# Block sums of the second MLP matrix moved into the first matrix's stage, and the first token group issued earlier

## The chip, the cores and the metric

The kernel runs on one core of one Trainium2 chip. The metric is the device time of one execution in microseconds. A core has TensorE (PE, matmuls; PEld is its weight load), VectorE (DVE), ScalarE (ACT), GpSimd (POOL) and SyncE (SP). In this kernel all transfers are issued on SP's queue, which issues them in order. Data lie in SBUF; matmuls write to PSUM, which has eight banks.

## The reference, cut to what matters

The kernel computes two layers of a token mixer, each followed by a dense MLP; the change is in the MLP and in what stands right before it.

```
def _sqrelu_mlp(h, w1, w2):
    return jnp.square(jax.nn.relu(h @ w1)) @ w2
...
for i in range(DEPTH):                       # DEPTH = 2
    ...                                      # mixer: short convolution (layer 0), mLSTM (layer 1)
    x = x + mx[2] * _rmsnorm(yx, nw[1])
    x = x + mx[5] * _rmsnorm(_sqrelu_mlp(_modulate(_rmsnorm(x, nw[2]), mx[3], mx[4]), mlp_w1[i], mlp_w2[i]), nw[3])
    if not last:
        ...                                  # the same for 256 context tokens
```

The model width is 1024, the MLP's inner width 4096. Layer 0 works on 1280 tokens (256 of context and 1024), layer 1 on 1024. All inputs are 32-bit floats.

## The kernel before

Every operand of a large matmul is split into a high and a low part (`fp32r`): ScalarE casts the value (the high part), VectorE subtracts the cast from it (the low part), and each product is three matmuls (`PASSES`: high-high, high-low, low-high). `piece` (L119) does this for a 128 x 512 weight piece: a cast at L122 and a subtraction at L123. The results go round a ring of eight slots.

Both MLP matrices use a 2 x 2 block product with seven block multiplications instead of eight (products numbered 1 to 7, used in the order 1, 6, 5, 7, then 2, 3, 4 in the first matrix's stage and 1, 6, 5, 7, 4, 2, 3 in the second's). For four of them (4, 5, 6, 7) the weight operand is a sum or difference of blocks of the matrix, and the activation operands are sums as well.

`out_proj` (L355) is the stage ahead of the MLP. For each tile of 128 tokens it multiplies by the output matrix, adds the normed result to the residual stream (`post_norm`, L283) and normalises again. For each pair of tiles `pre_norm2` (L323) transposes the result, applies scale and shift, forms the block sums (`sums`, L318 to L321) and writes the split parts into A0 or A1, the operands of the first MLP stage. A0 holds the first token group (384 token pairs in layer 0, 256 in layer 1), A1 the second (256). A1 lies where the output matrix lay, so the last two pairs' writes (`left`) are run after the stage.

`mlp_up` (L403) is the first matrix's stage. It takes the 4096 columns in 16 blocks q. For each it loads two tiles of w1 (512 KB each), forms four sums (L415, L416, L420, L425) in tiles `tw`, makes seven pieces, and for each of the two token groups runs seven products of 12 matmuls into the banks X, Y, Z, W. The banks are evicted by ScalarE (L447, L457) and VectorE (L449 to L459), squared-ReLU is applied on ScalarE, and VectorE forms the activation's four block sums. The tile `st` with seven parts goes to `hid_d` in DRAM (L465).

`mlp_down` (L468) is the second matrix's stage. For each of the seven products it makes a pass over 16 blocks k of w2's rows: `w_piece` loads blocks of w2 into a tile `raw` and, for products 4 to 7, forms the sum on VectorE (L485 for product 5, L490 and L491 for 6, L496 for 7, L500 for 4); product 6 stores its sum to `t2_d`, from which product 4 starts. `h_piece` loads the activation part from `hid_d` (`hr`, two buffers) and splits it (L509, L510). One step multiplies the piece with all token pairs (L515): five pairs in layer 0, four in layer 1, each into a PSUM bank of its own. At a pass's end `evict` empties the banks; there are six of them. The norms that follow (`done`, `finish`) are worked off between the steps.

The order of instructions on each engine and of DMAs on SP is fixed at build time by a scheduler: it follows program order where the operands of an instruction are expected to be ready. SBUF tiles lie in pools on two stacks, left and right; a tile in a newly opened pool waits until the older tiles at its address are no longer used. `raw` tiles come from a pool of three.

Of the kernel before, what the change touches and what calls it, by code (L numbers as in the profile page):

```python
# [37 lines left out]
def hybrid_kernel(  # L38
# [46 lines left out]
    t2_d = tc.dram_tile([2, DFF // P // 2, P, 512], F32, name="t2_d")  # L85
# [196 lines left out]

    def post_norm(ys, xsrc, G, T):  # L283
        xt = T.tile([P, D], F32, tag="xt", name="xt", bufs=hold["xt"])
        nc.sync.dma_start(xt, xsrc)
        tt = T.tile([P, D], F32, tag="tmp", name="tt", bufs=hold["tt"])
# [10 lines left out]
        return xt, tt  # L297
# [25 lines left out]
    def pre_norm2(xns, t, l, T, tp):  # L323
# [3 lines left out]
        def rest(A, c0):  # L327
            for k0 in range(0, 4, 2):
                val = T.tile([P, 4, 2, P], F32, tag="xt", name="val2", bufs=hold["xt"])
                S = T.tile([P, 4, 2, P], F32, tag="xt", name="S2", bufs=hold["xt"])  # L330
                for kk in range(2):
# [16 lines left out]
                for src, i0, n in ((val, 0, 3), (S, 3, 4)):  # L348
                    d = A[:, i0 : i0 + n, :, k0 : k0 + 2, c0 : c0 + P]
                    nc.scalar.copy(d[:, :, 0], src[:, 0:n])  # L350
                    nc.vector.tensor_sub(d[:, :, 1], src[:, 0:n], d[:, :, 0].bitcast(F32))
# [3 lines left out]
    def out_proj(l, zsrc, held, wsrc, tiles, xsrc, xdst, T, Z, acc, tp, G, A, early):  # L355
        ws = [load_w(wsrc[k * P : (k + 1) * P, :]) for k in range(KD)]
        later, xns, left = None, [], []
        hold.update(xt=3, tt=4)
        for t in tiles:
# [23 lines left out]
            xt, tt = post_norm(ps, xsrc(t), G(t), T)  # L383
# [7 lines left out]
            if len(xns) == 2:  # L391
                i = (t - tiles[0]) // 2
                rest = pre_norm2(xns, t - 1, l, T, tp)
# [5 lines left out]
        return later, left  # L399
# [3 lines left out]
    def mlp_up(l, As, M, acc):  # L403

        for q in range(NQ):
            raw = []
            for j in range(2):
                r = rawp.tile([P, 1024], F32, tag="raw", name="raw")
                nc.sync.dma_start(r, w1[l, 2 * q + j])
                raw.append(r)  # L410
            (b11, b21), (b12, b22) = [(r[:, 0:512], r[:, 512:1024]) for r in raw]
            ts = lambda: M.tile([P, 512], F32, tag="tw", name="tw", bufs=3)
            w = {1: piece(b11)}
            t1, t2 = ts(), ts()
            nc.vector.tensor_sub(t1, b12, b11)  # L415
# [754 lines left out]
```

## Time and profile before

| | us |
|---|---|
| median of three runs | 2706.17 (2695.35 to 2712.82) |
| the profiled execution's own time | 2706.2 |
| its span, first to last instruction | 2704.4 |
| TensorE busy in the span | 2577.7 (95%) |
| VectorE, ScalarE busy | 1665.5 (62%), 1157.0 (43%) |
| first MLP stage, layers 0 and 1 (with the change-over before it) | 532 to 953, 1982 to 2331 |
| second MLP stage, layers 0 and 1 | 953 to about 1390, 2331 to 2704 |

The busy time of TensorE is that of overlapping matmuls with modelled ends, so 95% does not say that it runs at its best rate; the number of matmuls in a stretch says more. PEclk is the granted clock of TensorE as a share of full speed.

### The profile page before, as it was taken

The page shows a single profiled execution, that of the slowest core. Times are in us where ns is not written, and L with a number is a line of the kernel's source. Part 1 is how long each engine was busy: PE and PEld are TensorE (multiplying, and loading weights), DVE is VectorE, ACT ScalarE, POOL GpSimd, SP SyncE. Part 2 cuts the span into 40 slices and gives each one's busy share as a digit, 9 for nine tenths or more (in the row PEclk, how much of TensorE's full clock was granted, in tenths as well). Part 3 has the DMA queues.
Part 4 walks back from the last instruction along what each step waited for, and adds up shares of the span by engine and source line. Part 5 has one row for each costly group of instructions (what it writes and reads, how often), then busy time and mean ns, then how long its engine had stood idle before and what let it go on. Part 6 is the DMA issues. An engine that isn't in the chain of part 4 may idle for free.

```text
span 2704.4 us, 38658 instructions
## 1 busy us (share of the span) xinstructions
PE 2577.7 (95%) x14520; PEld 2235.4 (83%) x14520; DVE 1665.5 (62%) x3020; ACT 1157.0 (43%) x2529; POOL 98.1 (4%) x223
## 2 busy tenths in 40 slices
PE   8999999989999998999999999999979999988998
PEld 6888787789999976787888778787869999866776
DVE  6677875665565555766657553544566666556765
ACT  6211113554444432435554543435555555423343
POOL 1000001100000000001020000000100000000010
PEclk9999999989999999999999999799989999989999
DMA  7466644333443388876633222213424444678875
GB/s 285 130 195 188 207 145 132 126 97 118 150 146 125 120 268 253 286 244 220 218 104 81 70 67 59 57 42 95 131 84 141 138 153 144 210 251 272 260 244 191
DMA packets 225021, 435.97 MB, mean 161 GB/s; under 512 B 17226, under 2 KB 108666, under 8 KB 224834
## 3 DMA queue, kind: packets, MB, share of 16 engines
q1 hardware_dynamic: 224834, 433.51, 50.1%
q8 instruction: 114, 1.87, 0.3%
q14 instruction: 73, 0.60, 0.1%
HBM read 333.07 MB, written 100.16 MB: 160 GB/s over the span
## 4 chain that ended last, share of the span: by engine, by line
PE 52%; issue 30%; DMA 9%; DVE 6%; ACT 2%; POOL 1%; SPq 0%; DVEq 0%; POOLq 0%; ACTq 0%
PE op L374 7%; PE psd L515 7%; PE psZ L432 4%; PE psW L432 4%; PE psX L432 4%; PE psv L842 4%; PE pso L129 3%; DMA raw<-in_w_dram 3%; DMA mraw<-in_mod_w_dram 3%; PE psc L129 3%; DMA Dm<-nm_d 2%; PE psb L129 2%; PE psu L129 2%; PE psY L432 2%; PE po L1009 1%
## 5 line engine op out<-in xcount | busy, mean ns | idle before, releaser
L515 PE MATMUL psd<-w,hp 128*128 128x512 f32 x3024 | 735.2, 404 | 47.6 <-ACT w L122 25.4
L515 PEld LDWEIGHTS psd<-w,hp 128*128 128x128 f32 x3024 | 579.2, 193 | 199.9 <-ACT w L122 31.5
L122 ACT CAST w<-raw 128x512 fp32r<-128x512 f32 x320 | 197.0, 619 | 225.7 <-DVE raw L491 67.8
L123 DVE TENSOR_TENSOR w<-raw,w 128x512 fp32r<-128x512 f32 x320 | 218.7, 688 | 98.3 <-ACT w L122 94.2
L509 ACT CAST hp<-hr 128x512 fp32r<-128x512 f32 (+1 forms) x226 | 150.6, 669 | 237.1 <-DMA hr<-hid_d 128.5
L432 PE MATMUL psX<-A,w 128*128 128x256 f32 (+1 forms) x1536 | 229.2, 298 | 14.3 <-ACT p L447 14.3
L432 PE MATMUL psZ<-A,w 128*128 128x256 f32 (+1 forms) x1536 | 228.2, 298 | 0.0
L432 PE MATMUL psW<-A,w 128*128 128x256 f32 (+1 forms) x1536 | 226.5, 297 | 0.0
L432 PEld LDWEIGHTS psX<-A,w 128*128 128x128 f32 x1536 | 213.6, 190 | 15.1 <-ACT p L447 15.1
L510 DVE TENSOR_TENSOR hp<-hr,hp 128x512 fp32r<-128x512 f32 (+1 forms) x226 | 168.5, 749 | 88.7 <-ACT hp L509 87.6
L432 PEld LDWEIGHTS psZ<-A,w 128*128 128x128 f32 x1536 | 214.4, 190 | 0.0
L432 PEld LDWEIGHTS psW<-A,w 128*128 128x128 f32 x1536 | 212.8, 189 | 0.0
L374 PE MATMUL op<-w,zs 128*128 128x512 f32 x864 | 205.4, 397 | 2.0 <-ACT zs L368 1.8
L374 PEld LDWEIGHTS op<-w,zs 128*128 128x128 f32 x864 | 162.0, 189 | 38.9 <-ACT zs L368 2.5
L220 DVE SCALAR_TENSOR_TENSOR macc<-mraw,sil,macc 128x1024 f32<-128x1024 f32 x112 | 140.4, 1280 | 39.6 <-DMA mraw<-in_mod_w_dram 39.3
L462 ACT ACTIVATE st<-st 128x256 f32<-128x256 f32 (+1 forms) x128 | 56.9, 445 | 224.9 <-DVE st L453 179.7
L109 ACT CAST w<-raw 128x1024 fp32r<-128x1024 f32 (+1 forms) x73 | 75.4, 1039 | 161.7 <-PE psc L129 54.9
L842 PE MATMUL psv<-w,hT 128*128 128x256 f32 (+1 forms) x960 | 142.3, 301 | 0.9 <-ACT val L270 0.9
L842 PEld LDWEIGHTS psv<-w,hT 128*128 128x128 f32 x960 | 128.2, 198 | 7.5 <-issue 1.8
L110 DVE TENSOR_TENSOR w<-raw,w 128x1024 fp32r<-128x1024 f32 (+1 forms) x73 | 87.6, 1208 | 70.5 <-ACT w L109 70.2
L432 PE MATMUL psY<-A,w 128*128 128x256 f32 (+1 forms) x768 | 116.9, 302 | 2.4 <-ACT w L122 2.4
L129 PE MATMUL psc<-hT,w 128*128 128x512 f32 (+1 forms) x576 | 114.4, 350 | 0.6 <-DVE hT L279 0.4
(241 smaller groups left out, 3582.0 us busy)
## 6 DMA issues: line engine op xcount, KB each, us to landing
raw<-in_w_dram SPq DMA_DIRECT2D x128, 512.0 KB, 4.7
raw<-in_w_dram SPq DMA_DIRECT2D x224, 256.0 KB, 3.9
hid_d<-st SPq DMA_DIRECT2D x48, 896.0 KB, 4.1
mraw<-in_mod_w_dram SPq DMA_DIRECT2D x80, 512.0 KB, 4.0
hr<-hid_d SPq DMA_DIRECT2D x104, 320.0 KB, 3.6
hr<-hid_d SPq DMA_DIRECT2D x122, 256.0 KB, 3.7
hid_d<-st SPq DMA_DIRECT2D x16, 1344.0 KB
xd<-xt SPq DMA_DIRECT2D x26, 512.0 KB, 2.7
```

Of the source, the lines that this page charges most:

```text
L109: nc.scalar.copy(w[0], src)
L110: nc.vector.tensor_sub(w[1], src, w[0].bitcast(F32))
L122: nc.scalar.copy(w[:, 0], src)
L123: nc.vector.tensor_sub(w[:, 1], src, w[:, 0].bitcast(F32))
L129: nc.tensor.matmul(ps, w[a][:, k * P : (k + 1) * P], hold["hT"][:, k, b, t0 : t0 + n], start=(k == 0 and i == 0), stop=(k == KD - 1 and i ...
L220: nc.vector.scalar_tensor_tensor(ac[v], raw, s, ac[v], ALU.mult, ALU.add)
L374: nc.tensor.matmul(ps[h], zs[:, a, k, :], ws[k][b][:, h * 512 : (h + 1) * 512], start=(k == 0 and i == 0), stop=(k == KD - 1 and i == 2),)
L432: nc.tensor.matmul(ps, w[i][:, a, k * P : (k + 1) * P], A[:, PIECE[i], b, k, :], start=(first and k == 0 and j == 0), stop=(k == 3 and j = ...
L509: nc.scalar.copy(h[:, 0], r)
L510: nc.vector.tensor_sub(h[:, 1], r, h[:, 0].bitcast(F32))
L515: nc.tensor.matmul(ps, h[:, a, o : o + P], w[:, b], start=(first and j == 0), stop=(last and j == 2))
L842: nc.tensor.matmul(ps[:, 0 : self.g], hold["hT"][:, k, a_, t * P : (t + 1) * P], self.wv[k // self.per][b_][:, k % self.per * self.g : (k ...
```

## The change

The first matrix's stage gets a second task. After each block q a new function `down_sums` loads the four blocks k = q of w2 (two tiles of 512 KB, one buffer each), forms the four sums for products 4 to 7 on VectorE and stores them to DRAM (`t_d`, 1 MB per block). `w_piece` in the second stage then only loads 256 KB, from w2 or from `t_d`, and makes the piece. `hr` has three buffers instead of two.

`mlp_up` is cut into `up_weights`, `up_group` and `down_sums`. The first block's first token group is issued before the `left` writes into A1; these now work on half-size tiles (m=1: one instead of two feature blocks at a time) in two buffers of a pool X of their own. The temporaries of that first group (pool M0) lie where `out_proj`'s pool T lay, which is closed earlier, since the normed tiles (`tt`) now lie in X. In `up_weights` two of the four sums are written over the loaded blocks, and `tw` has two buffers. In `up_group` the temporaries p1, u2, u4 and c21 are parts of `st`. In the last block the second group is run before the first.

```
-            for k0 in range(0, 4, 2):
-                val = T.tile([P, 4, 2, P], F32, tag="xt", name="val2", bufs=hold["xt"])
-                S = T.tile([P, 4, 2, P], F32, tag="xt", name="S2", bufs=hold["xt"])
-                for kk in range(2):
+            for k0 in range(0, 4, m):
+                val, S = [pl.tile([P, 4, m, P], F32, tag=tag, name=nm) for nm in ("val2", "S2")]
+                for kk in range(m):
...
+            tt = X.tile([P, D], F32, tag="xn", name="tt", bufs=4)
+            xt = post_norm(ps, xsrc(t), G(t), T, tt)
...
-                    later = lambda rest=rest, i=i: rest(A, i * P)
+                    later = lambda rest=rest, i=i: rest(A, i * P, T, "xt", 2)
                 else:
-                    left.append(lambda A, rest=rest, i=i: rest(A, (i - early) * P))
+                    left.append(lambda A, rest=rest, i=i: rest(A, (i - early) * P, X, "vs", 1))
...
+    def up_weights(l, q, M):
...
+        t2, t3 = [M.tile([P, 512], F32, tag="tw", name="tw", bufs=2) for _ in range(2)]
+        w = {1: piece(b11)}
+        nc.vector.tensor_sub(t3, b22, b12)
+        nc.vector.tensor_sub(b12, b12, b11)
+        nc.vector.tensor_sub(t2, b22, b12)
+        w[6] = piece(t2)
+        w[5] = piece(b12)
+        w[7] = piece(t3)
+        w[2] = piece(b21)
+        w[3] = piece(b22)
+        nc.vector.tensor_sub(b21, b21, t2)
+        w[4] = piece(b21)
...
+    def up_group(l, q, w, A, n, c0, M, acc):
...
+        st = M.tile([P, 7, n], F32, tag="st7", name="st7")
+        r11, r12, r22, c21, u2 = [st[:, i] for i in (0, 1, 2, 5, 6)]
...
+        prod(X, 1, True)
+        nc.scalar.copy(u2, X)
+        prod(Y, 6, True)
+        add(u2, Y, u2)
...
+    def down_sums(l, k, M):
+
+        r = []
+        for j in range(2):
+            r.append(M.tile([P, 1024], F32, tag=f"rw{j}", name="rw", bufs=1))
+            nc.sync.dma_start(r[j], w2[l, (2 * k + j) * P : (2 * k + j + 1) * P, :])
+        (b11, b12), (b21, b22) = [(x[:, 0:512], x[:, 512:1024]) for x in r]
+        t3 = M.tile([P, 512], F32, tag="tw", name="t3", bufs=2)
+        sub = nc.vector.tensor_sub
+        sub(t3, b22, b12)
+        sub(b12, b12, b11)
+        sub(b22, b22, b12)
+        sub(b21, b21, b22)
+        nc.sync.dma_start(t_d[l, k, :, 3], t3)
+        nc.sync.dma_start(t_d[l, k, :, 2], b12)
+        nc.sync.dma_start(t_d[l, k, :, 0:2], r[1].rearrange("p (a b) -> p a b", a=2))
+
+    def mlp_up(l, As, sX, left, acc):
+
+        (A0, n0), (A1, n1) = As
+        with pool("M0", bufs=1, side="right") as M:
+            w = up_weights(l, 0, M)
+            up_group(l, 0, w, A0, n0, 0, M, acc)
+            for f in left:
+                f(A1)
+        sX.close()
+        with pool("M", bufs=2, side="right") as M:
+            up_group(l, 0, w, A1, n1, n0, M, acc)
+            down_sums(l, 0, M)
+            for q in range(1, NQ):
+                w = up_weights(l, q, M)
+                both = [(A0, n0, 0), (A1, n1, n0)]
+                for A, n, c0 in both if q < NQ - 1 else both[::-1]:
+                    up_group(l, q, w, A, n, c0, M, acc)
+                down_sums(l, q, M)
...
         def w_piece(i, k):
-            raw = lambda: rawp.tile([P, 1024], F32, tag="raw", name="raw2")
             row = lambda j: w2[l, (2 * k + j) * P : (2 * k + j + 1) * P, :]
-            r = raw()
-            if i in (1, 2, 3):
...
-            o = r[:, 512:1024]
-            if i == 5:
-                nc.sync.dma_start(r, row(0))
-                nc.vector.tensor_sub(o, o, r[:, 0:512])
-            elif i == 6:
-                nc.sync.dma_start(r, row(0))
-                e = raw()[:, 0:512]
-                nc.sync.dma_start(e, row(1)[:, 512:1024])
-                nc.vector.tensor_sub(o, e, o)
-                nc.vector.tensor_add(o, o, r[:, 0:512])
-                nc.sync.dma_start(t2_d[l, k], o)
...
-            return piece(o)
+            src = {1: row(0)[:, 0:512], 2: row(1)[:, 0:512], 3: row(1)[:, 512:1024]}
+            r = rawp.tile([P, 1024], F32, tag="raw", name="raw2")[:, 0:512]
+            nc.sync.dma_start(r, src[i] if i in src else t_d[l, k, :, {4: 0, 6: 1, 5: 2, 7: 3}[i]])
+            return piece(r)
...
-            r = H.tile([P, NP * P], F32, tag="hr", name="hr", bufs=2)[:, 0:n]
+            r = H.tile([P, NP * P], F32, tag="hr", name="hr", bufs=3)[:, 0:n]
```

## Rows read from the trace of the kernel before

**Rows 1.** Busy time of each engine on the page, whole span, share and instructions
```profile
PE 2577.7 (95%) x14520; PEld 2235.4 (83%) x14520; DVE 1665.5 (62%) x3020; ACT 1157.0 (43%) x2529; POOL 98.1 (4%) x223
```

**Rows 2.** Stretches: start:end, length, busy of each engine, clock, DMA share, GB/s; first stage
```profile
582.00:952.00 370.00, 370.00 (x2512) 370.00 (x2511) 216.54 (x429) 176.72 (x371) 0.00 (x0) 1.00 0.40 134
...
2028.00:2330.00 302.00, 302.00 (x2519) 302.00 (x2519) 199.97 (x430) 165.71 (x373) 0.00 (x0) 1.00 0.45 147
```

**Rows 3.** Stretches of the second matrix's stage, both layers
```profile
953.30:1253.50 300.20, 284.60 (x1190) 225.24 (x1190) 182.51 (x269) 109.68 (x174) 0.00 (x0) 0.98 0.79 258
...
1017.00:1085.00 68.00, 57.89 (x230) 43.89 (x231) 35.32 (x51) 19.80 (x33) 0.00 (x0) 0.97 0.82 258
...
2330.60:2602.50 271.90, 244.37 (x967) 191.60 (x966) 170.27 (x265) 101.24 (x174) 0.00 (x0) 0.94 0.80 257
...
2335.00:2345.00 10.00, 10.00 (x31) 7.83 (x32) 3.81 (x6) 2.80 (x5) 0.00 (x0) 0.70 0.78 246
...
2382.00:2453.00 71.00, 54.51 (x190) 40.23 (x189) 37.30 (x56) 19.75 (x34) 0.00 (x0) 0.88 0.78 244
...
2506.00:2554.00 48.00, 46.60 (x192) 37.11 (x192) 35.01 (x56) 20.35 (x34) 0.00 (x0) 0.96 0.84 275
...
2554.00:2602.50 48.50, 46.58 (x192) 37.01 (x192) 33.33 (x53) 20.58 (x36) 0.00 (x0) 0.96 0.74 234
...
2562.00:2602.00 40.00, 40.00 (x174) 32.35 (x172) 24.83 (x40) 17.94 (x32) 0.00 (x0) 1.00 0.79 251
```

**Rows 4.** Waits in 2382 to 2453: who for whom, us in total, times, longest
```profile
DVE raw L490 <- DMA raw<-in_w_dram: 18.5, 10, 3.2
...
ACT w L122 <- DVE raw L491: 17.2, 11, 4.4
...
PE psd L515 <- ACT w L122: 15.4, 7, 3.5
```

**Rows 5.** Stretches from the output projection's last matmul, both layers
```profile
531.90:557.60 25.70, 10.49 (x52) 7.85 (x50) 19.73 (x33) 18.80 (x34) 2.08 (x5) 0.64 0.05 21
...
557.60:582.10 24.50, 24.50 (x154) 24.49 (x155) 15.31 (x28) 11.09 (x23) 0.00 (x0) 0.90 0.36 112
...
1981.60:2007.40 25.80, 10.07 (x54) 7.92 (x53) 19.75 (x33) 18.64 (x34) 2.09 (x5) 0.65 0.05 21
...
2007.40:2028.00 20.60, 20.56 (x149) 20.55 (x150) 14.02 (x28) 10.04 (x23) 0.00 (x0) 0.85 0.38 119
```

**Rows 6.** Groups of VectorE instructions: shapes, count, busy us, mean ns, idle before
```profile
L425 DVE TENSOR_TENSOR tw<-raw,tw 128x512 f32<-128x512 f32 x32 | 21.8, 681 | 0.0
...
L320 DVE TENSOR_TENSOR S<-val 128x256 f32<-128x256 f32 x18 | 7.6, 420 | 1.0 <-ACT val L340 0.2
```

**Rows 7.** DMA issues in 533:957, 2010:2331, 2382:2453: count, KB each, us to landing
```profile
hid_d<-st SPq DMA_DIRECT2D x15, 896.0 KB, 4.1
...
raw<-in_w_dram SPq DMA_DIRECT2D x28, 512.0 KB, 4.8
...
t_d<-raw SPq DMA_DIRECT2D x13, 256.0 KB, 3.8
```

**Rows 8.** Timeline: start, us, instruction; end of layer 1's first block, and DMA issues
```profile
2016.55 1.60 PE L432 MATMUL psW<-A,w 128*128 128x256 f32 x12
...
2021.66 0.38 SPq L465 DMA_DIRECT2D hid_d<-st  x1
...
2025.33 2.04 SPq L409 DMA_DIRECT2D raw<-in_w_dram  x2
```

**Rows 9.** Timeline at the start of layer 1's first stage (in brackets: idle before)
```profile
1989.41 0.75 DVE L389 TENSOR_SCALAR tt<-xt,rstd 128x1024 f32<-128x1024 f32 x1 [0.72 <-POOL rstd L242]
...
2004.35 1.86 PE L432 MATMUL psX<-A,w 128*128 128x256 f32 x7 [7.08 <-ACT p L447]
...
2005.32 0.69 DVE L415 TENSOR_TENSOR tw<-raw 128x512 f32<-128x512 f32 x1
...
2008.68 2.42 PE L432 MATMUL psY<-A,w 128*128 128x256 f32 x10
```

More of the change, by code (lines that the diff above doesn't have):

```diff
@@ L353, in pre_norm2, with out_proj @@
         return rest
-    def out_proj(l, zsrc, held, wsrc, tiles, xsrc, xdst, T, Z, acc, tp, G, A, early):
+    def out_proj(l, zsrc, held, wsrc, tiles, xsrc, xdst, T, X, Z, acc, tp, G, A, early):
         ws = [load_w(wsrc[k * P : (k + 1) * P, :]) for k in range(KD)]
         later, xns, left = None, [], []
-        hold.update(xt=3, tt=4)
         for t in tiles:
@@ new lines, in up_group, with prod @@
+    def up_group(l, q, w, A, n, c0, M, acc):
+        def prod(ps, i, first):
+            for k in range(4):
+                for j, (a, b) in enumerate(PASSES):
+                    nc.tensor.matmul(
+                        ps,
+                        w[i][:, a, k * P : (k + 1) * P],
+                        A[:, PIECE[i], b, k, :],
+                        start=(first and k == 0 and j == 0),
+                        stop=(k == 3 and j == 2),
+                        skip_group_check=not first,
+                    )
+        bank = lambda nm: acc.tile([P, 512], F32, tag="acc", name=nm)[:, 0:n]
+        st = M.tile([P, 7, n], F32, tag="st7", name="st7")
+        r11, r12, r22, c21, u2 = [st[:, i] for i in (0, 1, 2, 5, 6)]
+        X, Y, Z, W = bank("psX"), bank("psY"), bank("psZ"), bank("psW")
+        add = nc.vector.tensor_add
+        prod(X, 1, True)
+        nc.scalar.copy(u2, X)
+        prod(Y, 6, True)
+        add(u2, Y, u2)
+        prod(Z, 5, True)
+        add(r22, Z, u2)
+        prod(W, 7, True)
+        add(r22, W, r22)
+        prod(X, 2, False)
+        prod(Z, 3, False)
+        prod(W, 4, False)
+        nc.scalar.activation(r11, X, AF.Relu)
+        add(r12, Z, u2)
+        add(c21, W, u2)
+        nc.scalar.activation(r11, r11, AF.Square)
+        for c in (r22, r12, c21):
+            nc.scalar.activation(c, c, AF.Relu)
+            nc.scalar.activation(c, c, AF.Square)
+        add(st[:, 3], c21, r22)
+        nc.vector.tensor_sub(st[:, 4], st[:, 3], r11)
+        nc.vector.tensor_sub(st[:, 5], r11, c21)
+        nc.vector.tensor_sub(st[:, 6], r12, st[:, 4])
+        nc.sync.dma_start(hid_d[l, :, q, :, c0 : c0 + n].rearrange("s p n -> p s n"), st)
@@ L1086, in hybrid_kernel @@
         A1 = pA1.tile([P, 7, 2, 4, 256], F32R, name="A3")
-        for f in left:
-            f(A1)
-        sT.close()
-        with pool("M2", bufs=1, side="right") as M:
-            mlp_up(1, ((A0, 256), (A1, 256)), M, acc)
+        mlp_up(1, ((A0, 256), (A1, 256)), sX, left, acc)
     sA.close()
```

130 lines of the change are left out of this document (31 added, 99 removed).

## The prediction

> **What bounds the kernel now.** I read the busy line of the page first. TensorE is busy for 95% of the span and no other engine for more than 62% [rows 1], so time can only come from stretches where TensorE stands or runs at its lower clock. Next I cut the span by stage and then by pass. A view of stretches gives for each the busy time and count of each engine, the granted clock and the DMA share.
>
> The stages that compute the first MLP matrix are full: 302.0 of 302.0 us in the steady part of layer 1 and 370.0 of 370.0 in layer 0, clock 1.00, VectorE busy 200.0 and 216.5 us, DMA share 0.45 and 0.40 [rows 2]. Work that is put there and uses VectorE and the DMA queue finds room; work taken from there brings nothing.
>
> The second matrix's stage is not full. It has seven passes in the order 1, 6, 5, 7, 4, 2, 3, each of 16 steps. A pass issues 16 x 3 matmuls for each token pair: 240 in layer 0 (five pairs), 192 in layer 1 (four). At full clock with nothing missing one costs 40.00/174 = 0.230 us [rows 3], so a pass should take 55.2 and 44.1 us. Pass 6 takes 68.0 and 71.0 us, with granted clocks of 0.97 and 0.88 [rows 3]. In layer 1's pass 6 the longest wait of TensorE is 15.4 us for ScalarE's cast of the weight piece; that cast waits 17.2 us for VectorE's add that ends the block sum, and VectorE's subtraction ahead of the add waits 18.5 us for the weight load [rows 4]. So one chain sets the pass: three blocks loaded, two sums, cast, remainder, matmul. In bytes the same: a step of pass 6 moves 512 + 256 + 256 KB of weights beside the activations, against 256 KB in pass 1.
>
> The third place is the change from the output projection to the first MLP stage. From its last matmul to the end of the first block's second token group takes 50.2 us in layer 0 and 46.4 us in layer 1; in the first 25.7 and 25.8 us of it TensorE is busy for 10.5 and 10.1 at a clock near 0.65, VectorE for 19.7 [rows 5]. The two groups need only 12 x 7 matmuls each, 24.7 and 20.1 us at the steady rates (370.0 and 302.0 us over 15 blocks [rows 2]).
>
> **Part 1: block sums made early.** Removed from each step k of the second matrix: one subtraction (pass 5), a subtraction and an addition (6), one subtraction each (7, 4), with their larger loads. Each becomes one 256 KB load from t_d. Five VectorE instructions of 0.681 us [rows 6] go, 16 x 5 x 0.681 = 54 us per layer, but VectorE is not what ends here; the gain is the stall. From the end of the first stage's matmuls to the end of pass 4, layer 0 takes 300.2 us and layer 1 271.9 [rows 3]. Five passes at 0.230 us are 275.9 and 220.7, so 24.3 and 51.2 us are lost.
>
> What stays lost: passes 7 and 4 of layer 1, which show no DMA chain, take 48.0 and 48.5 us, 4 more than the floor, at a clock of 0.96 [rows 3]. That is the hand-over of PSUM banks at a pass's end, which the change leaves. I keep 4 us for each of the three hand-overs 6-5, 5-7, 7-4, 1 us for 1-6 and 2 us at the start: 15 in layer 1. In layer 0, with longer passes, I keep 4 in all. Saved: 36 + 20 = 56 us. Bounds: everything, 75; or pass 6 alone brought to its floor plus one us, 26 + 12 = 38.
>
> The start is in this sum: after the first stage TensorE now stands and then runs at a mean clock of 0.70 for 10 us, 31 matmuls where 43 would fit [rows 3]. The last block now takes its second group first, so that group's operand, under whose address the activation buffers lie by the order of the pools, comes free one group earlier, and the first loads run under the last group.
>
> **Part 2: what the first stage takes on.** Per block: two loads of 512 KB, four subtractions, stores of 256, 256 and 512 KB. VectorE gets 15 x 4 x 0.681 = 41 us in each steady stretch: 200 + 41 = 241 of 302 in layer 1, 257 of 370 in layer 0 [rows 2, 6]. DMA gets 2 MB per block, 31 MB in 302 us, so 147 + 104 = 251 GB/s; the second stage moves 257 GB/s at a share of 0.80 [rows 3] with passes that run full. Cover: TensorE's own 20.1 us per block. I cost it at nothing, and keep 10 us for the range.
>
> Two new waits. The sums' two load tiles exist once, so block k+1's loads wait for block k's stores: 2.0 us to issue two plus 4.8 us (load), 4 x 0.68 (sums), 3.8 plus about 1 us (stores) make about 14 us [rows 6 to 8], against 20.1 us per block. The other is the result tile: its first write is now the copy of product 1, about 1.4 us into a group, where before it was the third sum. The store is issued 3.5 us after its group's last matmul [rows 8] and lands 4.1 us later [rows 7], so at 7.6 us, while the next copy comes at 10.0 + 1.4 = 11.4. Behind that copy on ScalarE wait the casts of the next pieces, and TensorE itself not before the fifth product. Both fit.
>
> The Trainium skill, DMA: Bandwidth & Descriptors, section Latency and other measured facts, speaks against this: it gives 0.2 us for an HBM access on average and 2 us at high load. As an estimate by that page, 1.8 us more on each leg would make the cycle near 18 us and the store 9.4: still inside, so by page and by row the sum keeps its zero. No stretch of the trace shows the first stage under such a load.
>
> **Part 3: first token group ahead of the last norm.** Before, the sums of the first block wait for the norm's tiles to be released: the first subtraction starts at 2005.32, the norm's product stands 7.08 us on a copy, and ten matmuls then take 2.42 us, twice the 1.2 they take at full clock [rows 9]. After, the temporaries lie where the projection's tiles lay, free about when the last tile's normalisation ends (1989.41 + 0.75) [rows 9], so the first group can run at once. But the second group needs the same norm, and VectorE now has the group's work ahead of it. Until the second group's first product VectorE needs the 19.7 us of the first stretch [rows 5], four sums and four remainders (5.5 us), nine evictions and sums (0.55 us each for 384 elements, 0.42 for 256: 5.0 us in layer 0, 3.8 in layer 1), and more for the norm cut in half: by 0.420 us for 256 and 0.681 for 512 elements [rows 6], eight rounds of 4 x 0.29 + 0.55 + 0.68 are 19 us against four of 4 x 0.42 + 0.94 + 1.20, 15. The extra 14 us overlap by a tenth, so 32 and 31 us. If VectorE never stands, the second group ends six products (8.5 us) later, at 41 and 40; at the busy share it has there now (0.77), near 50. Against 50.2 and 46.4 this is +9 to 0 and +6 to -4. I take the middle, 4 + 1 = 5 us. The two buffers of the halved norm make the slow end no less likely.
>
> **The sum.** 56 + 5 = 61 us. The profiled execution spans 2704.4 us and its time is 2706.2, equal to the median of the runs shown. 2706 - 61 = 2645 us.
>
> **Rivals.**
> Best case: the whole loss of the second stage goes, 75 us, and VectorE runs through at the change of stage, 15: 2706 - 90 = 2616. For it: at clock 1.00 the long part of layer 1's pass 4 runs at the floor, 174 matmuls in 40.00 us; against it: the ends of passes 7 and 4 there [rows 3].
> The change does not cure pass 6: its stall comes with the activation loads, which share the queue. For it: ScalarE's cast of the activations idles on their loads too; against it: the bytes of those loads are the same in all passes, and pass 7 has TensorE busy for 46.6 of 48.0 us with them [rows 3]. Then only the start (12 us) and part 3 (5) stay: 2689.
> On the other side: the sums hold VectorE in the first stage. VectorE's order is fixed, so where a sum stands ahead of an eviction while its load is under way, it waits for the load. TensorE has about 2.9 us of cover (two products) before it needs that eviction. A wait of 4.8 us [rows 7] costs 2 us per block, 30 x 2 = 60: no gain. Both loads in series, 6.9, cost 4, 120 us: 2765. It makes the kernel over 1% slower from 5.8 us of waiting. Against it: now the same kind of wait, first subtraction on the w1 load, never stalls TensorE in those stretches. The skill's 2 us would bring it nearer.
>
> **How the numbers follow.** Forecast 0.65, best case 0.15, no cure 0.10, held VectorE 0.10. About 1% (27 us) is what a measurement can tell from no change. Faster than 2679: nearly all of the forecast, the best case, part of no cure: 0.80. Within 1%: 0.13. Slower: 0.07. The range runs from the best case, 2615, to the low bounds together (38 saved, 4 lost in part 3, 10 in part 2): 2682.
>
> **What would show it.** Right: all seven passes within 5 us of 55.2 and 44.1; no weight cast waiting on VectorE in pass 6; the first stage still full at clock 1.00 with VectorE near 0.70 and 0.80 busy and DMA near 250 GB/s; the first psd matmul within a us or two of the last first-stage matmul; the second group of the first block ending 41 to 50 us after the projection. Wrong: VectorE waiting on loads of w2, TensorE gaps once per block in the first stage, or a pass 6 still near 70 us.

## The result and the profile after

The changed kernel takes 2632.66 us (median of four runs, 2624.72 to 2644.35) against 2709.47 for the kernel before, measured beside it: a ratio of 0.973, with a 95% interval of 0.967 to 0.979. The forecast was 2645 us with a range of 2615 to 2682. The time fell by 74 us from the median of the runs shown at first and by 77 from the median measured beside it; 61 were forecast. The ratio's interval, 58 to 89 us, holds both, so only the lengths of the stages below tell the forecast's terms from what came. The profiled execution spans 2624.4 us (run time 2626.18), 80.0 less than that of before.

The busy line of the page after, beside [rows 1]:

```profile
PE 2549.2 (97%) x14520; PEld 2227.5 (85%) x14520; DVE 1634.4 (62%) x3036; ACT 1149.1 (44%) x2545; POOL 98.8 (4%) x223
```

Stretches of the changed kernel (start:end, length, busy of each engine, granted clock, DMA share, GB/s): the steady first stage and the whole second stage to the end of pass 4 in layer 0, the same in layer 1, then passes 6 and 4 of layer 1.

```profile
592.00:938.00 346.00, 346.00 (x2378) 346.00 (x2377) 238.11 (x469) 168.96 (x354) 0.00 (x0) 1.00 0.64 223
952.30:1228.40 276.10, 276.10 (x1191) 223.87 (x1190) 126.42 (x183) 103.38 (x169) 0.00 (x0) 1.00 0.57 180
...
2010.00:2300.00 290.00, 289.03 (x2434) 288.62 (x2433) 228.60 (x480) 157.39 (x363) 0.00 (x0) 1.00 0.74 252
2303.60:2525.00 221.40, 221.40 (x955) 179.53 (x954) 115.39 (x183) 96.87 (x172) 0.00 (x0) 1.00 0.66 205
2347.00:2391.50 44.50, 44.50 (x194) 36.06 (x193) 20.59 (x33) 20.11 (x36) 0.00 (x0) 1.00 0.63 189
2481.00:2525.40 44.40, 44.40 (x193) 36.00 (x192) 25.16 (x41) 19.10 (x34) 0.00 (x0) 1.00 0.60 191
```

TensorE now never stands in the second stage up to the end of pass 4, in either layer: 276.10 of 276.10 and 221.40 of 221.40 us, clock 1.00, where [rows 3] had 284.60 of 300.20 and 244.37 of 271.90. Pass 6 is an ordinary pass. The first stage stays full with the added work in it, with VectorE busy for 0.79 of it in layer 1 and 0.69 in layer 0, and the DMA moving 252 and 223 GB/s.

Where the 80 us went, by stage (us, from the timelines; the first stage runs from the output projection's last matmul to the second stage's first, in the kernel before to the last matmul of the first stage, so that its gap of about 4 us ahead of pass 1 counts to the second stage):

| stretch | before | after | gain |
|---|---|---|---|
| up to layer 0's last projection matmul | 532.1 | 529.2 | 2.9 |
| first stage, layers 0 and 1 | 421.2, 348.7 | 423.1, 349.5 | -1.9, -0.8 |
| second stage to the end of pass 4, layers 0 and 1 | 300.2, 271.9 | 276.3, 221.8 | 23.9, 50.1 |
| passes 2 and 3 of layer 0 up to that eviction; passes 2, 3 and what follows, layer 1 | | | 0.8, 2.8 |
| from the first eviction at the end of layer 0's pass 3 to layer 1's last projection matmul | 630.2 | 628.3 | 1.9 |

These add up to 79.7; the 0.3 us to 80.0 are rounding and where the stretches begin and end. Nearly all of the gain, 74.0 us, is the second stage; the first stage, where I had forecast 5 us of gain, lost 2.7.

### The profile page after: what moved, and what is told of

Same layout as the page of the kernel before. It is cut to its first block, busy times and chain, and to the rows that moved or that the text cites. A ratio compares the mean times of both kernels' runs of the same rounds, so it can differ in the third digit from the quotient of the medians.

```text
span 2624.4 us, 38836 instructions
## 1 busy us (share of the span) xinstructions
PE 2549.2 (97%) x14520; PEld 2227.5 (85%) x14520; DVE 1634.4 (62%) x3036; ACT 1149.1 (44%) x2545; POOL 98.8 (4%) x223
## 4 chain that ended last, share of the span: by engine, by line
PE 54%; issue 30%; DMA 7%; DVE 6%; ACT 2%; POOL 1%; SPq 0%; DVEq 0%; POOLq 0%; ACTq 0%
PE psd L528 11%; PE op L371 5%; PE psv L853 4%; PE psZ L429 4%; PE psW L429 4%; PE psX L429 4%; PE pso L129 3%; DMA mraw<-in_mod_w_dram 3%; PE psc L129 2%; PE psY L429 2%; DMA Dm<-nm_d 2%; PE psu L129 2%; PE psb L129 2%; PE po L1020 1%; DVE macc L220 1%
## 5 line engine op out<-in xcount | busy, mean ns | idle before, releaser
L528 PE MATMUL psd<-w,hp 128*128 128x512 f32 x3024 | 705.0, 395 | 0.0
L528 PEld LDWEIGHTS psd<-w,hp 128*128 128x128 f32 x3024 | 568.9, 188 | 132.2 <-DVE p L548 0.2
L123 DVE TENSOR_TENSOR w<-raw,w 128x512 fp32r<-128x512 f32 x384 | 261.1, 684 | 37.2 <-ACT w L122 36.8
L122 ACT CAST w<-raw 128x512 fp32r<-128x512 f32 x384 | 236.4, 617 | 95.9 <-DMA raw<-in_w_dram 31.4
L459 ACT ACTIVATE st<-st 128x256 f32<-128x256 f32 (+1 forms) x192 | 85.3, 444 | 247.7 <-DVE st L450 182.3
L109 ACT CAST w<-raw 128x1024 fp32r<-128x1024 f32 (+1 forms) x73 | 75.3, 1039 | 161.2 <-PE psc L129 60.9
L429 PE MATMUL psY<-A,w 128*128 128x256 f32 (+1 forms) x768 | 121.7, 305 | 13.2 <-ACT w L122 11.6
L429 PEld LDWEIGHTS psY<-A,w 128*128 128x128 f32 x768 | 111.3, 195 | 15.7 <-ACT w L122 12.4
```

The lines of the kernel that those rows point to most:

```text
L122: nc.scalar.copy(w[:, 0], src)
L123: nc.vector.tensor_sub(w[:, 1], src, w[:, 0].bitcast(F32))
L429: nc.tensor.matmul(ps, w[i][:, a, k * P : (k + 1) * P], A[:, PIECE[i], b, k, :], start=(first and k == 0 and j == 0), stop=(k == 3 and j = ...
L459: nc.scalar.activation(c, c, AF.Relu)
L528: nc.tensor.matmul(ps, h[:, a, o : o + P], w[:, b], start=(first and j == 0), stop=(last and j == 2))
```

## The experiments

All kernels below were profiled, and their stages are measured on the timelines in the same way; "first stage" here is the time from the output projection's last matmul to the second stage's first matmul, and "second stage" runs from there to the end of pass 4. Lengths are given as layer 0 / layer 1. The changed kernel has 423.1 / 349.5 and 276.3 / 221.8, the kernel before 425.4 / 353.0 and 296.2 / 267.7. Two executions of the changed kernel agree within 1 us in each of them (the second: 422.6 / 348.7 and 276.2 / 221.8), so a few microseconds are read from these lengths and not from whole times, which spread by 20 us here and by 45 in eleven executions of the kernel before (last section).

### The moved sums alone, and the other parts taken back one by one

**e1_sums_only** has parts 1 and 2 and no more: norm, order of the groups and two hr buffers as before.

```diff
-        with pool("M0", bufs=1, side="right") as M:
-            w = up_weights(l, 0, M)
-            up_group(l, 0, w, A0, n0, 0, M, acc)
-            for f in left:
...
+        for f in left:
+            f(A1)
+        sT.close()
...
-                for A, n, c0 in both if q < NQ - 1 else both[::-1]:
+                for A, n, c0 in both:
...
-                    left.append(lambda A, rest=rest, i=i: rest(A, (i - early) * P, X, "vs", 1))
+                    left.append(lambda A, rest=rest, i=i: rest(A, (i - early) * P, T, "xt", 2))
...
-  name="hr", bufs=3
+  name="hr", bufs=2
```

> Part 1 alone: the sums are made in the first stage and kept, but the norm and the first token group stand as in the kernel before, the last block takes its groups in the old order, and the activation loads keep two buffers. Theory A (the stall is the weight chain, and the sums also stood ahead of the evictions at the ends of the passes): from the end of the first stage to the end of pass 4 layer 0 takes 276 to 282 us and layer 1 222 to 228 (before 300.2 and 271.9), passes 7 and 4 lose their 4 us each too; only the start of a few us per layer stays; 2640 us in all. Theory B (pass 6 and the ends of the passes are cured by the third activation buffer): pass 6 of layer 1 stays above 60 us, 2670 or more.

Measured: 2640.84 us (four runs), ratio 0.976 (0.969 to 0.983). First stage 423.5 / 350.8, second stage 278.8 / 223.4; layer 1's passes 1, 6, 5, 7, 4 take 44.8, 44.8, 44.6, 44.6, 44.6. The moved sums alone cure every pass. All that TensorE still waits for in layer 1's second stage stands at its start; waits of TensorE there, in e1 (who for whom, us in total, times, longest):

```profile
PE psd L523 <- ACT hp L517: 4.5, 1, 4.5
```

**e2_hr2** takes the third hr buffer back.

```diff
-  name="hr", bufs=3
+  name="hr", bufs=2
```

> The changed kernel with two activation buffers instead of three. Theory A: passes 6, 5, 7, 4 stay within 2 us of the floor (55.2 and 44.1 us), the time as the changed kernel within 5 us. Theory B: TensorE waits at the ends of passes again, 2 to 4 us each in layer 1, 10 to 20 us in all.

Measured: one run, 2641.72 us; first stage 422.2 / 348.4, second stage 276.2 / 221.8, as in the changed kernel. Only layer 1's pass 2 differs: 49.5 us against 44.6, with one wait, of TensorE for an eviction (the same view, in that pass):

```profile
PE psd L528 <- DVE p L548: 2.6, 1, 2.6
```

The kernels with two hr buffers (before, e1, e2) take 49.1, 49.1 and 49.5 us in this pass; those with three that kept the early sums (after, e3, e4, and a second execution of the changed kernel) take 44.6, 45.8, 45.5 and 46.4. The buffer is worth about 3 to 5 us, in one place, and nothing in the passes that the change was about.

**e3_order** takes the reversed order of the last block back.

```diff
-                for A, n, c0 in both if q < NQ - 1 else both[::-1]:
+                for A, n, c0 in both:
```

> The changed kernel with the last block's groups in the old order. If the activation buffers wait for the second group's operand, TensorE stands about 4 us between the stages in both layers again and then runs some 10 us at a clock near 0.70: 6 us per layer, 12 in all. If the loads would be early enough anyway, the first matmul of the second stage follows within 1 us.

Measured: one run, 2638.84 us; first stage 427.4 / 351.4, second stage 278.0 / 225.0: 4.3 + 1.9 and 1.7 + 3.2 us, together 11.1, against the 12 that the rival without a cure set for the start. TensorE's timeline at the start of layer 1's second stage (start, us, instruction; in brackets the idle time before and its releaser), first in e3, then in the changed kernel:

```profile
2306.60 1.58 PE L429 MATMUL psW<-A,w 128*128 128x256 f32 x12
2312.68 12.53 PE L528 MATMUL psd<-w,hp 128*128 128x512 f32 x43 [4.49 <-ACT hp L522]
```

```profile
2302.21 1.58 PE L429 MATMUL psW<-A,w 128*128 128x256 f32 x12
2303.63 8.76 PE L528 MATMUL psd<-w,hp 128*128 128x512 f32 x37
```

In e3 43 matmuls take 12.53 us after the gap, where 9.9 would do at 0.230; with the order reversed there is no gap and 37 take 8.76, 0.237 each.

**e4_noearly** takes only the early group back; the norm keeps its halved tiles.

```diff
+        for f in left:
+            f(A1)
+        sX.close()
-        with pool("M0", bufs=1, side="right") as M:
-            w = up_weights(l, 0, M)
-            up_group(l, 0, w, A0, n0, 0, M, acc)
-            for f in left:
...
```

> Part 3 undone, the rest as changed (the norm still in two halves and two buffers): the last pairs' sums are written before the first block. By the forecast the early group is worth about 5 us in all. By the trace of the changed kernel, where block 1's pieces come late after the early group and TensorE stands 4.7 and 5.4 us there, it is worth between 0 and 5 us; the halved norm alone would cost some 6 us per layer against the kernel before, so from the projection's end to the second group's end 52 to 56 us in layer 0 and 48 to 52 in layer 1, with no late pieces in block 1.

Measured: 2629.77 us (four runs), ratio 0.973 (0.965 to 0.981), no longer than the changed kernel; but its first stage is 427.8 / 352.0, so the early group is worth 4.7 + 2.5 = 7.2 us, given the halved norm; 0 to 5 were expected. TensorE's largest wait in total at layer 1's change of stage in e4 is for the norm:

```profile
PE pt L335 <- ACT val L338: 13.2, 5, 4.5
```

In e1, with the whole norm, this row reads 7.5 us instead of 13.2. The lengths of the first stages of e1 and e4 can't be set side by side for this, since e1 also has the old order of the last block and stands some 4 us ahead of pass 1. When the stores of layer 0's and layer 1's second and fourth groups are issued, in us after the projection's last matmul, tells it more closely:

| kernel | group 2 | group 4 |
|---|---|---|
| before | 53.6 / 50.9 | 78.3 / 70.4 |
| e1 (sums, whole norm, no early group) | 52.6 / 49.4 | 77.4 / 70.1 |
| e4 (sums, halved norm, no early group) | 60.9 / 56.3 | 85.6 / 77.0 |
| after (early group) | 50.8 / 47.3 | 80.3 / 72.5 |
| e5 (early group, no sums) | 50.3 / 46.2 | 72.6 / 64.2 |
| e10 (early group, sums one block later) | 49.8 / 45.9 | 72.9 / 64.6 |

By group 4, e4 is 8.2 and 6.9 us behind e1: that is what the halved norm with its two buffers costs. With the early group the changed kernel makes up 5.3 and 4.5 us of it, not all. It does bring group 2 forward, by 2.8 and 3.6 us against before. One block later it is 2.0 and 2.1 us behind before. What happens in between is the next group of experiments.

### What the sums cost in the first stage

**e5_no_sums** leaves them out there.

```diff
-            down_sums(l, 0, M)
...
-                down_sums(l, q, M)
...
-  src[i] if i in src else t_d[l, k, :, {4: 0, 6: 1, 5: 2, 7: 3}[i]]
+  src.get(i, row(0)[:, 512:1024])
```

> The changed kernel with the sums of the second matrix left out (neither formed nor stored; passes 4 to 7 load 256 KB of w2 itself in their place, so the product is not the MLP's). What the sums cost in the first stage is the difference. By the forecast nothing: from the projection's end to the second stage 422 and 349 us as with them, within 3 us. If the first block's sums are what makes block 1's pieces late, 2 to 5 us less in each layer. If the stage were held by the loads, 30 us less in each.

Measured: one run, 2614.43 us; first stage 415.7 / 340.1, so the sums cost 7.4 + 9.4 = 16.8 us, where I had put nothing in the forecast and 2 to 5 in each layer before this run, and the second stage is the same (276.2 / 221.7). By the table 0.5 and 1.1 us of it have come by group 2, and 7.7 and 8.3 by group 4. TensorE's waits in layer 0 (529 to 952) and layer 1 (1954 to 2300) of the changed kernel, the rows on the weight pieces:

```profile
PE psY L429 <- ACT w L122: 4.7, 1, 4.7
```

```profile
PE psY L429 <- ACT w L122: 6.8, 2, 5.4
```

In e5 the same row of layer 1 reads 1.4 us. VectorE's timeline in the changed kernel, ahead of that wait, one cast on ScalarE, and TensorE's first matmuls after the wait:

```profile
1997.17 0.69 DVE L476 TENSOR_TENSOR t<-rw 128x512 f32<-128x512 f32 x1
...
1997.65 0.62 ACT L122 CAST w<-raw 128x512 fp32r<-128x512 f32 x1
...
1998.11 0.68 DVE L477 TENSOR_TENSOR rw<-rw 128x512 f32<-128x512 f32 x1
...
1998.71 0.68 DVE L411 TENSOR_TENSOR tw<-raw 128x512 f32<-128x512 f32 x1
...
1999.64 0.68 DVE L478 TENSOR_TENSOR rw<-rw 128x512 f32<-128x512 f32 x1
...
2001.25 0.68 DVE L479 TENSOR_TENSOR rw<-rw 128x512 f32<-128x512 f32 x1
...
2001.85 0.68 DVE L412 TENSOR_TENSOR raw<-raw 128x512 f32<-128x512 f32 x1
...
2003.06 0.68 DVE L413 TENSOR_TENSOR tw<-raw 128x512 f32<-128x512 f32 x1
...
2004.44 0.79 PE L429 MATMUL psY<-A,w 128*128 128x256 f32 x2 [5.41 <-ACT w L122]
```

Lines 476 to 479 are block 0's sums of w2, and 411 to 413 are block 1's sums of w1, from which its pieces are cut. The second kind stands between and behind the first kind and group 2's evictions. VectorE never idles between 1997.17 and the wait's end, and ScalarE has cast pieces straight from block 1's loaded tiles, the last at 1997.65, so the other pieces wait for VectorE's order and not for a load. In the steady stage TensorE has 20 us of matmuls per block under all this. Here VectorE has just done the norm, and the pieces of block 1 come late. TensorE stands, and as it starts again its clock falls to half (1.2 GHz); stretches of the changed kernel up to the wait and from it on, layer 0 and layer 1, and the 3 us from layer 1's first matmul after the wait:

```profile
529.40:576.10 46.70, 36.88 (x214) 34.78 (x214) 33.03 (x77) 28.43 (x61) 1.68 (x5) 0.85 0.27 86
576.10:592.00 15.90, 11.18 (x53) 10.52 (x52) 10.70 (x21) 4.86 (x10) 0.00 (x0) 0.79 0.73 256
1954.30:1997.40 43.10, 33.32 (x213) 31.03 (x212) 31.30 (x77) 27.52 (x61) 1.68 (x5) 0.80 0.25 83
1997.40:2010.00 12.60, 7.19 (x49) 6.97 (x49) 10.20 (x20) 4.71 (x10) 0.00 (x0) 0.86 0.74 251
2004.40:2007.40 3.00, 2.96 (x13) 2.94 (x14) 2.35 (x4) 0.62 (x1) 0.00 (x0) 0.50 1.02 280
```

**e6_dve2** gives VectorE four more subtractions per block, **e7_dma2** sends every w2 load and every t_d store twice.

```diff
-        sub(t3, b22, b12)
+        for _ in range(5):
+            sub(t3, b22, b12)
```

```diff
+            for _ in range(2):
                 nc.sync.dma_start(r[j], w2[l, (2 * k + j) * P : (2 * k + j + 1) * P, :])
...
+        for _ in range(2):
             nc.sync.dma_start(t_d[l, k, :, 3], t3)
...
```

> The changed kernel with the first subtraction of each block's sums made five times over (same result): VectorE gets 4 x 0.6 us more per block, 37 us per layer, and would be busy for some 265 of 290 us in layer 1's first stage. By the forecast (TensorE's own time covers it) layer 0 is unchanged and layer 1 loses less than 10 us. If VectorE's order and not its load counts, evictions come late and each block loses 1 to 2 us, 15 to 30 us per layer.

> The changed kernel with each load of w2 and each store of the sums in the first stage issued twice (same data): 4 MB more than the kernel before per block in place of 2, and the cycle of load, sums, store that runs through single buffers grows from about 14 us to about 25. By the forecast's working the cycle then exceeds layer 1's 20.1 us per block and the stage is held: 15 x 5 = 75 us more in layer 1, near 0 to 10 us in layer 0 (24.7 us per block). If there is more room than I thought, or transfers overlap, neither layer moves by more than 10 us.

Measured: e6 2631.43 us (one run), first stage 424.8 / 358.5, that is +1.7 / +9.0; e7 2679.95 us (one run), 424.2 / 407.5, +1.1 / +58.0 where 75 were expected for layer 1. Stretches of layer 1's first stage, e6 and then e7, and under them e7's waits there, of TensorE and of the DMA queue's engine:

```profile
2000.00:2290.00 290.00, 283.70 (x2341) 280.66 (x2340) 248.03 (x513) 146.61 (x348) 0.00 (x0) 1.00 0.70 238
```

```profile
2000.00:2340.00 340.00, 304.31 (x2382) 298.49 (x2382) 225.61 (x464) 152.35 (x352) 0.00 (x0) 0.95 0.86 294
```

```profile
PE psY L429 <- ACT w L122: 26.8, 14, 4.9
```

```profile
SPq L473 <- DMA rw<-in_w_dram: 41.7, 24, 3.5
SPq L473 <- DMA t_d<-rw: 36.9, 22, 3.8
```

So VectorE nearly has room for twice the sums in the steady stage: it is busy for 248 of 290 us, and TensorE loses 6. The transfers have no such room in layer 1. With each sent twice, a block takes longer than its matmuls: 58 us over 15 blocks, 3.9 each, makes 24 us per block against 20.1. In layer 0, where a block takes 24.7 us, it still fits. The run lengthens the chain of load, sum and store as well as doubling its bytes, since a tile's second load waits for the first to land (the 41.7 us above); which of the two sets the 24 us was not separated. The 294 GB/s are below the 310 that a pass of e8 reaches further down, which speaks for the chain.

**e10_shift** issues a block's sums behind the next block's weights. **e11_shift_vs4** has this too, and four buffers for the halved norm's tiles in layer 1; layer 0, with two as before, is its control.

```diff
-            down_sums(l, 0, M)
             for q in range(1, NQ):
                 w = up_weights(l, q, M)
+                down_sums(l, q - 1, M)
...
-                down_sums(l, q, M)
+            down_sums(l, NQ - 1, M)
```

```diff
-  val, S = [pl.tile([P, 4, m, P], F32, tag=tag, name=nm) for nm in ("val2", "S2")]
+  val, S = [pl.tile([P, 4, m, P], F32, tag=tag, name=nm, bufs=3 if m == 2 else 2 + 2 * l) for nm in ("val2", "S2")]
```

> The changed kernel with each block's sums of w2 issued behind the next block's weights. Without sums the way from the projection to the second stage took 415.7 and 340.1 us, with them 423.1 and 349.5. If the first block's sums cost by standing ahead of block 1's pieces, most of this comes back: 417 to 420 and 342 to 346 us, 10 us in all. If they cost wherever they stand, it stays at 423 and 349.

> As the run before, and in layer 1 the halves of the norm get four buffers instead of two (layer 0 has no room and is the control). The rounds of the norm take 2.97 us each in the changed kernel, in a chain through two buffers; with four, VectorE's and ScalarE's own time of about 2 us should set them: 4 to 6 us less in layer 1 than in the run before, layer 0 unchanged. 2618 to 2624 us in all, against 2633 for the changed kernel.

> The changed kernel itself, beside the two runs before it, for a comparison on one chip: 0.973 of the kernel before, 423 and 349 us between projection and second stage.

Measured in one comparison: before 2715.42 us (11 runs), the changed kernel again (**e12_changed_again**) 2627.69 (six, ratio 0.968, 0.964 to 0.973), e10 2611.68 (four, 0.962, 0.956 to 0.968), e11 2593.97 (six, 0.957, 0.952 to 0.962). First stages: e10 415.1 / 340.6, which is e5's 415.7 / 340.1 with all the sums made; e11 415.1 / 334.8. The 17 us were a matter of order: e10 moves the w2 loads and stores on SP's queue too, but the timeline above has VectorE's order as what the pieces waited for. The gain against e12, 7.5 + 8.1 = 15.6 us, is more than the 10 expected. The four buffers give 5.8 more in the one layer that has them. The change of stage in layer 1, e10 and then e11, with TensorE's wait on the pieces in e10 under it:

```profile
1950.30:2000.00 49.70, 39.61 (x278) 37.38 (x277) 40.99 (x97) 32.18 (x72) 1.68 (x5) 0.90 0.32 103
```

```profile
1964.00:2010.00 46.00, 40.07 (x299) 37.50 (x298) 41.76 (x101) 33.51 (x76) 1.70 (x5) 0.93 0.39 131
```

```profile
PE psY L429 <- ACT w L122: 1.7, 1, 1.7
```

In e10 VectorE is busy for 41 of 49.7 us and TensorE waits 1.7 us for a piece, where the changed kernel waited 5.4. Both e10 and e11 are faster than the two kernels compared; e11 is 33.7 us under the changed kernel, more than the two gains in its first stages (7.5 + 13.9 = 21.4 us against e12). Its time is also below the 2618 to 2624 us expected. What the rest is can't be read from a profile, but it goes with the clock: the one execution of e11 that was profiled took 2621.13 us at a mean granted clock of 0.979, the other five 2591.01 to 2595.36 at 0.991 to 0.994, and the six of e12 have 0.974 to 0.987 (last section).

### Late loads or the sums behind them

Pass 6 of before lost by loads that come late, by sums that wait for them on VectorE, or by both. Two kernels made from the kernel before separate these. **e8_loads_only** has all its loads and the store of t2 and no sums; **e9_subs_only** has its sums on VectorE, on one 256 KB load, and stores nothing; the edits of w_piece, e8's and then e9's.

```diff
-                nc.vector.tensor_sub(o, o, r[:, 0:512])
...
-                nc.vector.tensor_sub(o, e, o)
-                nc.vector.tensor_add(o, o, r[:, 0:512])
-                nc.sync.dma_start(t2_d[l, k], o)
+                nc.sync.dma_start(t2_d[l, k], e)
...
-                nc.vector.tensor_sub(o, o, r[:, 0:512])
...
-                nc.vector.tensor_sub(o, o, r[:, 0:512])
```

```diff
-            o = r[:, 512:1024]
-            if i == 5:
-                nc.sync.dma_start(r, row(0))
...
+            o, e = r[:, 512:1024], r[:, 0:512]
+            nc.sync.dma_start(e, row(0)[:, 0:512])
+            nc.vector.tensor_sub(o, e, e)
+            if i == 6:
+                nc.vector.tensor_add(o, o, e)
```

> The kernel before with the sums' loads and the store left as they are, but the sums themselves left out (the loaded block goes straight to the cast, so the product is not the MLP's). If the loads' bytes and number set pass 6, it stays above 65 us in layer 1; if the two VectorE sums in the chain do, it falls below 50 us. Passes 5, 7 and 4 end without a wait for evictions if it was the sums standing ahead of them: about 45 us instead of 52.9, 48.2 and 48.2.

> The counterpart of the loads-only run: the kernel before where passes 5, 6, 7 and 4 load one block of 256 KB, as pass 1 does, but still make their one or two VectorE sums (of that block with itself, so the product is not the MLP's; nothing is stored). With loads only, pass 6 of layer 1 took 61.8 us where before it took 70.9 and the floor is 44.1. If the two parts add, pass 6 falls to about 53 us here; if the sums only cost because their loads are late, to below 46. If the sums' place ahead of the evictions makes the waits at the ends, passes 7 and 4 stay at 48 us.

Measured: e8 2668.81 us (one run), second stage 291.1 / 253.3; e9 2658.2 us (one run), second stage 278.7 / 224.0. Stretches of e8's passes 6, 5 and 7 in layer 1, then of e9's passes 6 and 5:

```profile
2358.80:2420.60 61.80, 48.87 (x181) 36.26 (x182) 19.25 (x28) 18.77 (x32) 0.00 (x0) 0.92 0.83 259
2420.60:2467.50 46.90, 44.80 (x193) 36.05 (x192) 26.38 (x39) 21.65 (x35) 0.00 (x0) 1.00 0.92 310
2467.50:2517.50 50.00, 47.57 (x205) 38.29 (x203) 25.67 (x40) 21.47 (x36) 0.00 (x0) 1.00 0.90 291
```

```profile
2374.60:2418.90 44.30, 44.30 (x192) 35.93 (x191) 37.09 (x60) 20.26 (x37) 0.00 (x0) 1.00 0.63 201
2418.90:2463.50 44.60, 44.60 (x194) 36.16 (x193) 33.38 (x54) 18.45 (x32) 0.00 (x0) 1.00 0.60 189
```

Waits in e8's pass 6, and the timeline at the end of its pass 7 (in brackets: idle before):

```profile
ACT w L122 <- DMA raw<-in_w_dram: 19.8, 12, 2.8
...
PE psd L510 <- ACT w L122: 12.1, 7, 2.8
```

```profile
2515.74 0.62 ACT L122 CAST w<-raw 128x512 fp32r<-128x512 f32 x1 [1.54 <-DMA raw<-in_w_dram]
2516.39 0.69 DVE L123 TENSOR_TENSOR w<-raw,w 128x512 fp32r<-128x512 f32 x1 [1.38 <-ACT w L122]
...
2518.94 1.50 PE L510 MATMUL psd<-w,hp 128*128 128x512 f32 x3 [3.87 <-DVE u L525]
```

In e9 VectorE is busy for about the same time in pass 6 as in the kernel before (37.09 us, in 44.30 instead of 71.0), and passes 6, 5, 7 and 4 are within 0.6 us of the floor: the sums cost nothing where their loads are small. In e8 no sum is left, and pass 6 still takes 61.8 us, between the two forecasts: the cast waits for the load itself, 19.8 us, and TensorE for the cast, 12.1. Of the 26.8 us that the kernel before lost in this pass (70.9 against 44.1) the loads alone account for 17.7, and the rest needs both. VectorE as a cause by itself falls. The small losses at the ends of the later passes are there in e8 too (46.9 and 50.0 us), with the DMA share at 0.90 and above, and they are gone in e9. The timeline shows how a load makes them: the evictions of pass 7 stand on VectorE behind the remainder (L123) of a coming weight piece, which waits for its cast, and the cast waits for its load.

Why the loads come late was not taken apart. Bytes, the number of loads and the three `raw` tiles, of which pass 6 takes two per step, all change between before and e9. By bytes alone, as an estimate from the tiles' sizes: pass 6 of layer 1 moves 16 times 512 + 256 KB of weights, 256 KB of activations and the 256 KB of t2, 21 MB; at 310 GB/s, the most of any stretch shown here, that is 68 us. A part of it is loaded before the pass begins, so bytes would be enough for most of what e8 takes.

## Why the prediction was right, and where not

**What bounds it: right.** The time came from the second stage, and from loads that came late there. The chain of [rows 4] has the load as its first step, and e8 and e9 show that this step carries it.

**Part 1: the mechanism right, a term too small.** I took 56 us and gave everything, 75, as the upper bound; 74.0 came. The step that failed is "That is the hand-over of PSUM banks at a pass's end, which the change leaves. I keep 4 us". The hand-overs were not a cost of their own: with small loads TensorE runs across all of them (276.10 of 276.10 us). The 4 us at the ends of passes 7 and 4 [rows 3] came from the same loads: e8 has such losses without a single sum, e9 has sums and no losses. That they "show no DMA chain" was a misreading. TensorE's own waits there are for evictions, but the sums behind which these stand wait for loads; waits in passes 7 and 4 of layer 1, before (2506 to 2603):

```profile
DVE raw L500 <- DMA raw<-in_w_dram: 6.0, 5, 2.3
DVE raw L496 <- DMA raw<-in_w_dram: 5.7, 6, 1.4
```

**The start: right.** It was worth 11 us by e3; the rival without a cure had put it at 12. The first psd matmul now follows the last one of the first stage directly.

**The third hr buffer: not in the prediction.** It gives some 3 to 5 us in layer 1's pass 2 (e2).

**Part 2, steady stage: right.** I forecast 241 of 302 us (0.80) and 257 of 370 (0.70) for VectorE and 251 GB/s; 0.79, 0.69 and 252 GB/s in layer 1 came. The two new waits stayed hidden. Landing times of the transfers in layer 1's first stage after (issues, KB each, us to landing):

```profile
hid_d<-st SPq DMA_DIRECT2D x29, 896.0 KB, 5.1
rw<-in_w_dram SPq DMA_DIRECT2D x28, 512.0 KB, 5.8
raw<-in_w_dram SPq DMA_DIRECT2D x25, 512.0 KB, 4.0
```

The new loads of w2 take 1.0 us more than the 4.8 of a w1 load of that size before [rows 7], but the w1 loads themselves take 4.0, less than before. The 4.1 us of the store in [rows 7] are layer 0's, where it now takes 5.5. The cycle still fits its 20.1 us, and in e7, with every transfer sent twice, it does not. By the Trainium skill (DMA: Bandwidth & Descriptors, Latency and other measured facts) I had estimated 1.8 us more on each leg. The traces agree in the direction for the store and the new loads, with 1.4 and 1.0 us, and not for the loads of w1.

**Part 2 at the change of stage, and part 3: wrong in sign.** I forecast 5 us of gain for part 3 and nothing for the sums. The second group's last matmul ends 46.6 and 43.1 us after the projection, inside the 41 to 50 I gave, and 3.6 and 3.3 earlier than before [rows 5]: that step held. I stopped there. The next instructions on VectorE are block 0's sums and the evictions, and block 1's pieces stand behind them; TensorE waited 4.7 and 5.4 us for those pieces and then ran at a lower clock. "I cost it at nothing" took its cover from the steady stage, 20 us of matmuls per block, and there is no such cover while VectorE is catching up on the norm. By e3 against e1, which differ in part 3 (and in the hr buffers, which e2 shows not to matter there), part 3 as a whole cost 3.9 + 0.6 us in the first stage. Within it the halved norm costs 8.2 and 6.9 us by group 4, where I had counted 4 us of VectorE's work, and the early group, with the sums behind it, earns 5.3 and 4.5 back. Where the norm comes first the same sums cost little: TensorE's row on block 1's pieces reads 1.3 us in e1 and 0.8 in e4 (layer 1), and e1's groups 2 and 4 are issued no later than those of before, by the table. No run has the early group with the whole norm.

**Rivals.** The best case's first half came true, 74 of 75 us, its second half did not as the kernel stands. In e10 the first stages are 6.1 and 8.1 us shorter than before's, 14.2 of the 15 of that half, and its time (2611.68 us, beside 2715.42 for the kernel before) is near the best case's 2616. The held VectorE did not come: in the steady stage TensorE is busy for 346.00 of 346.00 and 289.03 of 290.00 us. The missing cure fell with pass 6 at 44.8 us.

**The sum.** 56 was 74; the 5 of part 3 was -2.7 together with all else in the first stage; 3.6 came in passes 2 and 3 and after, 4.8 in stages that the change doesn't touch. 61 forecast, 80 in the profiled executions, 74 and 77 in the medians. That the total came so near is in part luck: 18 us too little in part 1, 7.7 too much at the change of stage, and 8.4 from places without a term.

## What to carry to other kernels

A pass that loses a few microseconds at its ends while much is being loaded (a DMA share of 0.74 to 0.92 in the passes here) may owe them to the same loads as the pass that visibly stalls, so the floor at full clock is a better estimate of what remains than today's losses of the neighbouring passes. Work moved into a full stage is free only where the engine that does it has its slack; follow that engine's order through the start of the stage as well, past the first point that looks right, until the order is that of the steady state. Issue what is not needed soon behind what the next block needs: the same four subtractions cost 17 us ahead of the next block's weights and nothing behind them.

## What the runs showed of the hardware that I had not expected

The stretch from the end of layer 0's MLP (the first eviction at the end of pass 3) to the last matmul of layer 1's output projection is the same code in all these kernels, and it took 615 to 648 us from one execution to another. The stretch in three executions: before, e8, e11.

```profile
1351.70:1981.90 630.20, 613.34 (x3340) 508.74 (x3339) 325.70 (x794) 283.68 (x838) 45.24 (x91) 0.96 0.29 80
```

```profile
1345.00:1960.10 615.10, 594.63 (x3340) 494.07 (x3339) 325.11 (x794) 283.76 (x838) 45.18 (x91) 0.99 0.29 82
```

```profile
1315.80:1963.70 647.90, 631.21 (x3340) 521.69 (x3340) 326.43 (x794) 284.48 (x838) 45.94 (x91) 0.93 0.27 78
```

The counts are the same and VectorE's and ScalarE's busy times agree within 0.5%; what goes with the length is the granted clock, 0.99 to 0.93, of an engine that is busy for 97% of the stretch. The clock is not a little lower all along; it is at half, 1.2 GHz, in a few places. The longest of them before, ahead of which TensorE was busy for 2.55 of 4.00 us, and the same matmuls in e8, with 2.79 of 4.10 us busy ahead of them:

```profile
1730.10:1767.60 37.50, 37.50 (x135) 30.47 (x134) 12.02 (x42) 12.91 (x57) 1.89 (x2) 0.50 0.26 46
```

```profile
1725.60:1749.50 23.90, 22.08 (x134) 17.64 (x133) 11.27 (x42) 13.03 (x57) 1.83 (x2) 1.00 0.31 65
```

At half clock they take 37.5 us with TensorE busy all the time, at full clock 23.9 us with short waits between them. e11 has the fall at this place and another of 44.4 us some 106 us later, e8 neither; seven of the fourteen profiled executions have 37.5 us at half clock at this place. Why it comes in one execution and not in the next was not found. The spread is more than any part of the change but the first is worth: e4's time (2629.77) does not show the 7.2 us that its first stages lost.
